# Latent squares, key tiles, cross values and attention banks rearranged in a two-layer hybrid trunk

## The chip, the core and the metric

The kernel runs on one core of one Trainium2 chip. The metric is the device time of one execution in microseconds, and the value compared is the median of several runs. All arithmetic is in float32. A product of two matrices is made of three matmuls in the fp32r form: each operand is split into a high half and the rest, and high times high, high times low and low times high are added up in PSUM.

## What is computed

The reference is a decoder trunk of two layers over 512 tokens of width 1024, with a memory of 256 tokens. Cut to what matters:

```python
h = x
for l in range(2):
    h = h + hybrid_mixer(rmsnorm(h, attn_norm[l]), ...)
    h = h + memory_cross_attention(rmsnorm(h, cross_norm[l]), rmsnorm(mem, mem_norm[l]), ...)
    h = h + squared_relu_mlp(rmsnorm(h, mlp_norm[l]), mlp_w1[l], mlp_w2[l])
return rmsnorm(h, final_norm)

def hybrid_mixer(n, pos, ...):
    proj = n @ w_in          # c_q 256, c_kv 128, k_r 32, then q, k, v of 6 diff heads and of 4 moba heads
    qh  = rmsnorm(c_q, q_norm) @ w_uq        # 6 latent heads, 64 + 32 rotary
    kvh = rmsnorm(c_kv, kv_norm) @ w_ukv     # 64 key, 64 value columns a head
    k_a = concat(k part of kvh, rope(k_r))   # one rotary key for all heads
    o_a = causal_softmax(q_a, k_a) @ v
    lam = exp(sum(lq1*lk1)) - exp(sum(lq2*lk2)) + lam_init
    o_b = rmsnorm((softmax(q1,k1) - lam * softmax(q2,k2)) @ dv, sub_norm) * (1 - lam_init)
    o_c = moba_attention(...)                # with 512 tokens: causal over all blocks
    return concat(o_a, o_b, o_c) @ w_out
```

## The kernel before

The residual stream stands transposed in eight tiles `h` of 128 features x 512 tokens. Weights stream in from HBM through `fetch` (L151) and are split into two halves by `halve`: a copy on ScalarE (L157), the rest by a subtraction (L162) on GpSimd in the mixers, elsewhere wholly or by turns on VectorE. `weights` keeps two blocks ahead in the mixer.

A mixer has two kinds of work that `pipeline` interleaves. *Fill* steps are the projections, in the order "kv cq tok m0 d0 m1 d1 o0 m2 d2 o1 mem cross": the latents (kv, cq: `latent_steps`), the token products (tok: values of two diff pairs and the rotary key, `token_steps`), query, key and value of a latent pair (m: `mla_steps`) and of diff and moba pairs (d, o), and the memory's keys and values (`cross_memory_steps`). *Units* are the attention heads, four query blocks of 128 each, in the order "m0 d0 m1 d1 o0 m2 d2 o1". A unit makes its scores (L638 reads them with the mask or distance added, L640 is the exponent), two units later the probabilities are transposed (L280) and split (L660, L663), and after the last block `mix` (L679, L680 read its bank) multiplies them with the values. A diff head has two maps of scores a unit.

Work that must not stand at once in an engine's queue is put off in *ticks*: each eighth of a projection counts one, a token product 288/512, a latent pair's value and each of its two query products two, its key product one. `after(n, call)` makes the call n ticks later, so the ticks set the place of an instruction in program order. The planner of the framework then orders each engine's instructions by program order and by when it reckons them ready, so a later one may pass an earlier one. Transposes and single matmuls keep their order on TensorE (`hold`), the three matmuls of a product don't.

PSUM has three tags: "mm" with three banks (projections, latent products, cross values), "s" with three (scores, and by `ptags` the mix, tag "o"), "t" with two (transposes, column sums). The token products hold two "mm" and two "s" banks.

The latent query (cq) has two column blocks. Each is copied out (L760) and squared (L762) on ScalarE, the second square is added to the first on VectorE (L764), and `column_sums` multiplies the sum by ones, two columns wide, to get the sums per token. From them the norm's factor is made (GpSimd's power L339 among others), spread over rows by transposes, multiplied in (L782), and split; GpSimd writes the low half (L142).

At the eviction of the token products `rotate` turns the rotary key with seven small VectorE operations (L825 to L828). `turn` transposes it two ticks later, writes it to the first of four key tiles and sends it to three others by DMA (L843). `mla_steps` makes its key product only when the list of key tiles isn't empty. `setup_lambda` (L481 to L489, due at tick 58) reads lam by DMA, and the diff heads use the result. `setup_distances` is due from tick 24.

The cross values are two halves of eight weights each: for every weight the matmuls of both token tiles, each in a bank of its own, both evicted (L144, L145) at the half's end.

Of the kernel before, what the change touches and what calls it, by code (L numbers as in the profile page):

```python
# [101 lines left out]
class Trunk:  # L102
# [251 lines left out]
    def column_sums(self, sq, ones, ntok, w):  # L354

        o = self.psum("t")
        for j in range(ntok):
            self.mm(o[:, j * w:(j + 1) * w], sq[:, j * P:(j + 1) * P], ones, True, True)
        return o
# [10 lines left out]
    def rms_cols(self, sq, ntok, width, bufs, then=None):  # L370
        ms = self.column_sums(sq, self.ones2, ntok, 2)
# [101 lines left out]
    def setup_lambda(self):  # L473
        nc, const = self.nc, self.const
        v = self.tmp()
        nc.sync.dma_start(v[:, :L * 4 * 32], self.a["lam"].to_broadcast([P, L * 4 * 32]))
        prod, dots, ex = self.small(64), self.small(4), self.small(4)
        for l in range(L):
            for j in range(2):
                o = (l * 4 + 2 * j) * 32  # L480
                nc.vector.tensor_tensor(prod[:, :32], v[:, o:o + 32], v[:, o + 32:o + 64], ALU.mult)  # L481
                nc.vector.tensor_reduce(dots[:, 2 * l + j:2 * l + j + 1], prod[:, :32], mybir.AxisListType.X, ALU.add)
        nc.scalar.activation(ex, dots, AF.Exp)
        self.neg_lam = const.tile([P, L], F32, name="neg_lam")
        for l in range(L):
            li = 0.8 - 0.6 * math.exp(-0.3 * l)
            nl = self.neg_lam[:, l:l + 1]
            nc.vector.tensor_tensor(nl, ex[:, 2 * l + 1:2 * l + 2], ex[:, 2 * l:2 * l + 1], ALU.subtract)
            nc.vector.tensor_scalar_sub(nl, nl, li)  # L489
# [139 lines left out]
    def scores(self, i, terms, bias, slope):  # L629

        nc = self.nc
        n = (i + 1) * P
        s = self.psum("s")
        for j, (q, k) in enumerate(terms):
            self.mm(s[:, :n], q[:, i * P:n], k[:, :n], j == 0, j == len(terms) - 1, hold=False)
        t = self.tmp()
        st = self.small(2)
        nc.vector.tensor_tensor_reduce(out=t[:, :n], in0=s[:, :n], in1=bias, scale=-slope, scalar=TOP,  # L638
                                       op0=ALU.add, op1=ALU.min, accum_out=st[:, 0:1])
        nc.scalar.activation(t[:, :n], t[:, :n], AF.Exp, bias=st[:, 0:1], scale=-1.0, accum_out=st[:, 1:2])  # L640
        return t, st[:, 1:2]
# [45 lines left out]
    def head_units(self, maps, bias, slope, v, e, o, mixed, done=None):  # L687


        nc = self.nc  # L690
        st = {}

        def start(i):
            n = (i + 1) * P
            got = [self.scores(i, terms(), bias(i), slope) for terms in maps]
            t, sm = got[0]
            if len(maps) == 1:
                r = self.small(1)
                nc.vector.reciprocal(r, sm)
                (nc.gpsimd if i == 1 else nc.vector).tensor_scalar_mul(t[:, :n], t[:, :n], r)  # L700
            else:
                t2, s2 = got[1]
                nc.vector.scalar_tensor_tensor(t[:, :n], t2[:, :n], mixed(i, sm, s2), t[:, :n], ALU.mult, ALU.add)  # L703
# [38 lines left out]
    def mixer(self, l):  # L742
# [9 lines left out]
        def latent_steps(srcs, gain, width):  # L752


            cs = []
            sq = None
# [12 lines left out]
            def columns():  # L769
                ms = self.column_sums(sq, self.ones2, NQ, 2)  # L770
# [21 lines left out]
        def token_steps():  # L792

            n = 2 * P + 32
            ps = [self.psum("mm"), self.psum("mm"), self.psum("s"), self.psum("s")]
# [9 lines left out]
            def evict():  # L805
                vs = []
# [24 lines left out]
            def turn(t):  # L831
# [64 lines left out]
        def mla_units(p, got):  # L896
# [74 lines left out]
        def pair_units(p, got):  # L971
# [20 lines left out]
            def r1():  # L992
                if "r1" not in oo:
                    oo["r1"] = self.sb.tile([P, 2 * NQ], F32, tag="r1", name=self.name("r1"), bufs=2)
                return oo["r1"]

            def mixed(e):
                def factor(i, s1, s2):
# [3 lines left out]
                    nc.vector.reciprocal(r1()[:, 2 * i + e:2 * i + e + 1], s1)  # L1002
                    return r[:, 1:2]
                return factor

            def done_diff():

                ot, r = o(), r1()
# [3 lines left out]
                def columns():  # L1012
                    ms = self.column_sums(sq, self.halves, NQ, 2)
# [33 lines left out]
        self.keys = []  # L1047
# [121 lines left out]
    def cross_memory_steps(self, l):  # L1169
# [246 lines left out]
    def run(self):  # L1416
# [3 lines left out]
        self.ptags = {"o": "s"}  # L1420
# [11 lines left out]
        self.chain_n, self.chain_l, self.chain_d, self.chain_k = 6, 12, 4, 2  # L1432
# [135 lines left out]
```

## Time and profile before

| | |
|---|---|
| median of 3 runs | 1529.4 us (1529.02 to 1532.49) |
| profiled execution | 1527.16 us |
| its span, first to last instruction | 1525.3 us |
| TensorE busy | 1481.2 us, 97% |
| VectorE busy | 1060.3 us, 70% |
| ScalarE busy | 856.9 us, 56% |
| GpSimd busy | 365.3 us, 24% |
| mean granted TensorE clock | 0.994 |

Layer 0 runs to about 772 us and layer 1 from there. In each the mixer takes the first quarter thousand microseconds or so, then come the output projection, the cross attention and the feed-forward part. A row of the timeline gives the start and the length of a group of like instructions on one engine, and in brackets how long the engine stood idle before it and which instruction ended that.

### The profile page before, as it was taken

To read this page: it belongs to the slowest core of one execution; us is meant where nothing else is said; L and a number is where in the kernel's file an instruction comes from. 1 tells how busy PE (TensorE), PEld (TensorE's weight loads), DVE (VectorE), ACT (ScalarE), POOL (GpSimd) and SP (SyncE) were. 2 spreads that over 40 slices of the span, in tenths; PEclk is the share of its full clock that TensorE was granted. 3 is DMA by queue.
4 is the path that set the end of the run, shared out by engine and by line. 5 is a ranking of instruction groups with operands and counts; after the bars stand their busy time and mean duration, and the time that the engine had idled before them with its cause. 6 is when DMAs were issued, how large, how long until landed. Compare 5 with 4: busy or idle time off the path is not lost.

```text
span 1525.3 us, 24601 instructions
## 1 busy us (share of the span) xinstructions
PE 1481.2 (97%) x8648; PEld 1295.4 (85%) x8648; DVE 1060.3 (70%) x2422; ACT 856.9 (56%) x1887; POOL 365.3 (24%) x302
## 2 busy tenths in 40 slices
PE   7899999999999999999999999999999999999997
PEld 6778897888899899998897888878888989899887
DVE  7688888536699666675537898873378976677753
ACT  5666777535566544454446677764366654445441
POOL 2645375442000000000145446644400000000001
PEclk9999999999999999999999999999999999999998
DMA  4434543231223323322224535423212332333331
GB/s 153 127 106 138 153 132 111 77 96 49 87 74 125 111 88 105 100 96 98 96 77 112 150 113 154 118 86 95 98 34 76 106 123 90 104 96 106 111 97 55
DMA packets 90139, 157.24 MB, mean 103 GB/s; under 512 B 12065, under 2 KB 17057, under 8 KB 90017
## 3 DMA queue, kind: packets, MB, share of 16 engines
q1 hardware_dynamic: 89728, 155.63, 33.2%
q8 instruction: 68, 1.11, 0.3%
q14 instruction: 55, 0.44, 0.1%
q10 hardware_dynamic: 288, 0.05, 0.0%
HBM read 136.24 MB, written 2.10 MB: 91 GB/s over the span
## 4 chain that ended last, share of the span: by engine, by line
PE 71%; DVE 10%; issue 9%; ACT 4%; DMA 3%; POOL 2%; SPq 0%; POOLq 0%; DVEq 0%; ACTq 0%
PE mm L277 58%; PE s L277 10%; PE t L280 2%; DMA raw<-w 2%; DVE tmp L638 1%; ACT tmp L640 1%; DVE tmp L703 1%; POOL w L162 1%; DVE pt L663 1%; ACT B L140 1%; DMA raw<-w_in 1%; DVE small L1001 1%; POOL B L142 1%; PE t L277 1%; DVE tmp L261 1%
## 5 line engine op out<-in xcount | busy, mean ns | idle before, releaser
L277 PE MATMUL mm<-B,w 128*128 128x512 f32 (+1 forms) x2490 | 574.4, 386 | 1.3 <-POOL B L142 1.3
L277 PEld LDWEIGHTS mm<-B,w 128*128 128x128 f32 x2490 | 453.0, 189 | 95.1 <-POOL B L142 2.6
L277 PE MATMUL mm<-A,w 128*128 128x512 f32 (+1 forms) x1920 | 386.7, 351 | 6.2 <-ACT A L144 5.8
L157 ACT CAST w<-raw 128x512 fp32r<-128x512 f32 (+1 forms) x372 | 225.1, 607 | 269.6 <-PE mm L277 208.0
L277 PEld LDWEIGHTS mm<-A,w 128*128 128x128 f32 x1920 | 311.8, 190 | 50.7 <-ACT A L144 5.8
L162 POOL TENSOR_TENSOR w<-raw,w 128x512 fp32r<-128x512 f32 (+2 forms) x180 | 228.0, 1273 | 220.1 <-ACT w L157 177.9
L410 POOL TENSOR_TENSOR tmp<-tmp,tmp 128x512 f32<-128x512 f32 (+1 forms) x25 | 30.8, 1234 | 655.7 <-ACT tmp L407 653.6
L162 DVE TENSOR_TENSOR w<-raw,w 128x512 fp32r<-128x512 f32 x192 | 134.4, 700 | 35.5 <-ACT w L157 35.2
L640 ACT ACTIVATE tmp<-tmp,small 128x384 f32<-128x384 f32 (+3 forms) x176 | 99.0, 562 | 66.0 <-DVE small L638 63.2
L1080 DVE TENSOR_TENSOR h<-mm,h 128x512 f32<-128x512 f32 x92 | 63.3, 688 | 70.9 <-PE mm L277 70.6
L140 ACT CAST B<-tmp 128x512 fp32r<-128x512 f32 (+2 forms) x156 | 91.9, 591 | 24.1 <-DVE tmp L680 4.8
L277 PE MATMUL mm<-pt,B 128*128 128x256 f32 x768 | 102.9, 283 | 2.4 <-ACT tmp L1319 2.4
L277 PEld LDWEIGHTS mm<-pt,B 128*128 128x128 f32 x768 | 95.8, 189 | 3.4 <-ACT tmp L1319 3.4
L261 DVE TENSOR_TENSOR tmp<-raw,raw 128x512 f32<-128x512 f32 x64 | 44.0, 688 | 65.9 <-DMA raw<-w 65.9
L264 ACT CAST B<-tmp 128x512 fp32r<-128x512 f32 x96 | 59.5, 620 | 50.8 <-DVE tmp L261 50.8
L142 DVE TENSOR_TENSOR B<-tmp,B 128x512 fp32r<-128x512 f32 (+1 forms) x110 | 75.5, 686 | 12.3 <-ACT B L140 8.3
L280 PE MATMUL t<-ident,tmp 128*128 128x128 f32 (+1 forms) x444 | 74.5, 274 | 9.3 <-DVE tmp L828 3.3
L280 PEld LDWEIGHTS t<-ident,tmp 128*128 128x128 f32 (+1 forms) x444 | 54.2, 140 | 24.8 <-issue 4.2
L142 POOL TENSOR_TENSOR B<-tmp,B 128x512 fp32r<-128x512 f32 (+1 forms) x46 | 61.4, 1340 | 49.7 <-ACT B L140 47.4
L663 DVE TENSOR_TENSOR pt<-t,pt 128x256 fp32r<-128x256 f32 (+1 forms) x192 | 67.1, 370 | 6.3 <-ACT pt L660 5.4
L277 PE MATMUL s<-pt,B 128*128 128x512 f32 (+3 forms) x352 | 71.0, 345 | 0.0
L339 POOL TENSOR_TENSOR small<-small,mhalf 128x4 f32<-128x4 f32 (+2 forms) x19 | 23.4, 1229 | 198.2 <-DVE small L373 174.5
(195 smaller groups left out, 2135.8 us busy)
## 6 DMA issues: line engine op xcount, KB each, us to landing
raw<-w SPq DMA_DIRECT2D x256, 256.0 KB, 2.9
raw<-w_in SPq DMA_DIRECT2D x64, 256.0 KB, 3.0
st<-B SPq DMA_DIRECT2D x144, 64.0 KB, 2.0
raw<-w_ck SPq DMA_DIRECT2D x32, 256.0 KB, 2.9
raw<-w_cv SPq DMA_DIRECT2D x32, 256.0 KB, 2.7
raw<-w_out SPq DMA_DIRECT2D x32, 256.0 KB, 2.7
raw<-w_cq SPq DMA_DIRECT2D x32, 256.0 KB, 2.7
raw<-w_co SPq DMA_DIRECT2D x32, 256.0 KB, 2.6
```

The lines of the kernel that those rows point to most:

```text
L140: nc.scalar.copy(hi, x)
L142: eng.tensor_tensor(lo, x, hi.bitcast(F32), ALU.subtract)
L157: self.nc.scalar.copy(w[:, 0, :], raw)
L162: eng.tensor_tensor(w[:, 1, :], raw, w[:, 0, :].bitcast(F32), ALU.subtract)
L261: nc.vector.tensor_tensor(got[name], x, y, op)
L264: nc.scalar.copy(w[:, 0, :], raw)
L277: self.in_order(self.nc.tensor.matmul(out, lhs, rhs, start=start, stop=stop, skip_group_check=open), hold)
L280: self.in_order(self.nc.tensor.transpose(out, x, self.ident))
L410: eng.tensor_tensor(s[:, :n], s[:, :n], self.sq[:, :n], ALU.add)
L640: nc.scalar.activation(t[:, :n], t[:, :n], AF.Exp, bias=st[:, 0:1], scale=-1.0, accum_out=st[:, 1:2])
L663: nc.vector.tensor_tensor(lo, src, hi.bitcast(F32), ALU.subtract)
L1080: nc.vector.tensor_tensor(self.h[m], ps, self.h[m], ALU.add)
```

## The change

- `column_sums` takes a list of square tiles and adds them up in PSUM; the latents hand over both squares and the add on VectorE goes.
- `setup_lambda` works on all pairs at once and is due at tick 44 instead of 58; the distances are due from tick 28 instead of 24.
- The exponent's sums of the first map of a diff head go straight to the tile that held their reciprocals; one reciprocal of eight columns is taken when the pair is done.
- The multiply of the probabilities of block 1 runs on VectorE instead of GpSimd.
- The token products use three "s" banks and one "mm" bank.
- The four key tiles are allocated at the eviction of the token products; the turn comes six ticks after the rotation instead of two, and a latent head's scores wait, in program order, for the turn.
- In the cross values the second token tile runs two weights behind the first.
- The mix takes a bank of tag "mm" instead of "s".

```diff
-    def column_sums(self, sq, ones, ntok, w):
+    def column_sums(self, sqs, ones, ntok, w):
         o = self.psum("t")
         for j in range(ntok):
-            self.mm(o[:, j * w:(j + 1) * w], sq[:, j * P:(j + 1) * P], ones, True, True)
+            for i, sq in enumerate(sqs):
+                self.mm(o[:, j * w:(j + 1) * w], sq[:, j * P:(j + 1) * P], ones, i == 0, i == len(sqs) - 1)
...
-        prod, dots, ex = self.small(64), self.small(4), self.small(4)
-        for l in range(L):
-            for j in range(2):
-                o = (l * 4 + 2 * j) * 32
-                nc.vector.tensor_tensor(prod[:, :32], v[:, o:o + 32], v[:, o + 32:o + 64], ALU.mult)
-                nc.vector.tensor_reduce(dots[:, 2 * l + j:2 * l + j + 1], prod[:, :32], mybir.AxisListType.X, ALU.add)
+        prod, dots, ex = self.small(128), self.small(4), self.small(4)
+
+        pairs = v[:, :L * 4 * 32].rearrange("p (g f d) -> p g f d", f=2, d=32)
+        prod = prod.rearrange("p (g d) -> p g d", d=32)
+        nc.vector.tensor_tensor(prod, pairs[:, :, 0, :], pairs[:, :, 1, :], ALU.mult)
+        nc.vector.tensor_reduce(dots, prod, mybir.AxisListType.X, ALU.add)
...
-        st = self.small(2)
+        st = self.small(1)
...
-        nc.scalar.activation(t[:, :n], t[:, :n], AF.Exp, bias=st[:, 0:1], scale=-1.0, accum_out=st[:, 1:2])
-        return t, st[:, 1:2]
+        nc.scalar.activation(t[:, :n], t[:, :n], AF.Exp, bias=st[:, 0:1], scale=-1.0, accum_out=sums)
+        return t
...
-                (nc.gpsimd if i == 1 else nc.vector).tensor_scalar_mul(t[:, :n], t[:, :n], r)
+                nc.vector.tensor_scalar_mul(t[:, :n], t[:, :n], r)
...
                 s = self.tmp()
                 nc.scalar.activation(s, c, AF.Square)
-                if sq is not None:
-                    nc.vector.tensor_tensor(s, s, sq, ALU.add)
-                sq = s
+                sqs.append(s)
                 cs.append(c)
...
-                ms = self.column_sums(sq, self.ones2, NQ, 2)
+                ms = self.column_sums(sqs, self.ones2, NQ, 2)
...
-            ps = [self.psum("mm"), self.psum("mm"), self.psum("s"), self.psum("s")]
+            ps = [self.psum(t) for t in ("s", "s", "s", "mm")]
...
             def evict():
+                self.keys += [self.pair("B") for _ in range(4)]
...
-                first = self.pair("B")
+                first = self.keys[0]
                 self.split(first[64:128, 0, :], first[64:128, 1, :], u[64:128, :], kind="kr")
-                self.keys.append(first)
-                for j in range(3):
-                    kt = self.pair("B")
+                for kt in self.keys[1:]:
                     nc.sync.dma_start(kt[64:128].bitcast(F32), first[64:128].bitcast(F32))
-                    self.keys.append(kt)
+                self.turned = True
...
                 def terms(e=e):
+                    while not self.turned:
+                        self.tick()
...
-                    nc.vector.reciprocal(r1()[:, 2 * i + e:2 * i + e + 1], s1)
...
-                ot, r = o(), r1()
+                ot, r = o(), self.small(8)
+                nc.vector.reciprocal(r, sums())
...
             ps = [self.psum("mm") for t in range(2)]
-            for k in range(KT):
-                w = self.weights(a["w_cv"][l, c * KT + k])
-                for t in range(2):
-                    ts = slice(t * P, (t + 1) * P)
-                    self.mm3(ps[t], (mem[k][0][:, ts], mem[k][1][:, ts]), (w[:, 0, :], w[:, 1, :]),
-                             k == 0, k == KT - 1)
-                    yield 640
+            ws = []
+            for j in range(KT + 2):
+                if j < KT:
+                    ws.append(self.weights(a["w_cv"][l, c * KT + j]))
+                for t, k in ((0, j), (1, j - 2)):
+                    if 0 <= k < KT:
+                        ts, w = slice(t * P, (t + 1) * P), ws[k]
+                        self.mm3(ps[t], (mem[k][0][:, ts], mem[k][1][:, ts]), (w[:, 0, :], w[:, 1, :]),
+                                 k == 0, k == KT - 1)
+                        yield 640
...
-        self.ptags = {"o": "s"}
+        self.ptags = {"o": "mm"}
...
-        self.chain_n, self.chain_l, self.chain_d, self.chain_k = 6, 12, 4, 2
+        self.chain_n, self.chain_l, self.chain_d, self.chain_k = 6, 12, 4, 6
...
-            self.after(24 + 2 * n, part)
-        self.after(58, self.setup_lambda)
+            self.after(28 + 2 * n, part)
+        self.after(44, self.setup_lambda)
```

## Rows read from the trace of the kernel before

**Rows 1.** Page, part 1: busy us (share of the span), instructions by engine.

```profile
PE 1481.2 (97%) x8648; PEld 1295.4 (85%) x8648; DVE 1060.3 (70%) x2422; ACT 856.9 (56%) x1887; POOL 365.3 (24%) x302
```

**Rows 2.** TensorE's waits, whole span: us in total, times, longest.

```profile
PE s L277 <- DVE small L638: 4.1, 6, 1.2
PE s L277 <- DVE tmp L680: 3.4, 7, 0.7
PE t L280 <- DVE tmp L828: 3.3, 2, 2.4
PE t L277 <- DVE tmp L764: 2.9, 1, 2.9
...
PE t L280 <- DVE tmp L700: 2.4, 1, 2.4
...
PE mm L277 <- DVE B L145: 2.2, 2, 1.1
...
PE t L280 <- POOL tmp L700: 1.2, 1, 1.2
```

**Rows 3.** Stretches: us, PE, PEld, DVE, ACT, POOL busy, PEclk, DMA share, GB/s.

```profile
40.50:42.00 1.50, 1.50 (x8) 1.50 (x7) 1.49 (x4) 1.10 (x2) 0.85 (x1) 0.50 0.15 57
...
39.00:44.00 5.00, 5.00 (x29) 5.00 (x28) 3.83 (x10) 2.48 (x5) 3.40 (x4) 0.66 0.27 69
76.50:81.50 5.00, 5.00 (x18) 4.20 (x19) 4.63 (x14) 2.13 (x6) 1.01 (x1) 0.66 0.32 76
807.00:812.00 5.00, 5.00 (x18) 4.01 (x18) 2.39 (x4) 2.97 (x5) 2.56 (x2) 0.66 0.31 82
```

**Rows 4.** TensorE's timeline, first 60 us: start, us, instructions [idle before <-releaser].

```profile
29.43 0.67 PE L277 MATMUL mm<-w,A 128*128 128x288 f32 x3 [0.67 <-ACT tmp L760]
...
37.29 1.02 PE L277 MATMUL t<-ones,tmp 128*128 128x2 f32 x8 [2.86 <-DVE tmp L764]
...
51.06 0.97 PE L277 MATMUL mm<-B,w 128*128 128x512 f32 x3 [0.71 <-POOL B L142]
52.32 2.11 PE L277 MATMUL mm<-B,w 128*128 128x512 f32 x8 [0.29 <-POOL B L142]
```

**Rows 5.** TensorE by line and shape, two-column sums: count | busy us, mean ns.

```profile
L277 PE MATMUL t<-ones,tmp 128*128 128x2 f32 x92 | 11.1, 241 | 4.6 <-DVE tmp L764 2.9 <-DVE tmp L410 1.7
```

**Rows 6.** ScalarE's timeline, 18 to 58 us.

```profile
32.88 0.63 ACT L762 ACTIVATE tmp<-tmp 128x512 f32<-128x512 f32 x1
```

**Rows 7.** GpSimd's timeline, 18 to 58 us.

```profile
49.74 2.53 POOL L142 TENSOR_TENSOR B<-tmp,B 128x512 fp32r<-128x512 f32 x2
```

**Rows 8.** VectorE's timeline, 56 to 84 us.

```profile
71.27 0.19 DVE L481 TENSOR_TENSOR small<-tmp 128x32 f32<-128x32 f32 x1 [1.39 <-DMA tmp<-lam]
...
73.92 0.69 DVE L638 CUSTOM_DVE_ANT_0 tmp<-s,causal 128x512 f32<-128x512 f32 x1
```

**Rows 9.** VectorE's timeline, 797 to 822 us.

```profile
802.80 0.22 DVE L826 TENSOR_TENSOR tmp<-tmp,nsin 128x64 f32<-128x64 f32 x1
...
803.08 1.32 DVE L827 TENSOR_TENSOR tmp<-tmp,tmp 128x64 f32<-128x64 f32 x1
...
820.22 1.39 DVE L700 TENSOR_SCALAR tmp<-tmp,small 128x384 f32<-128x384 f32 x1
```

**Rows 10.** GpSimd's timeline, 797 to 822 us.

```profile
802.96 1.36 POOL L162 TENSOR_TENSOR w<-raw,w 128x512 fp32r<-128x512 f32 x1 [0.68 <-ACT w L157]
...
820.11 1.29 POOL L142 TENSOR_TENSOR B<-tmp,B 128x512 fp32r<-128x512 f32 x1 [0.28 <-ACT B L140]
```

**Rows 11.** The same view, the mixers' 25 us in which VectorE is fullest.

```profile
175.00:200.00 25.00, 24.07 (x161) 21.59 (x161) 22.94 (x66) 18.71 (x50) 14.51 (x12) 1.00 0.68 189
```

**Rows 12.** TensorE's timeline, 222 to 275 us.

```profile
231.14 1.48 PE L277 MATMUL s<-pt,B 128*128 128x512 f32 x8
```

**Rows 13.** VectorE's timeline, 222 to 275 us.

```profile
235.92 0.69 DVE L680 TENSOR_TENSOR tmp<-s,tmp 64x512 f32<-64x512 f32 x1
```

More of the change, by code (lines that the diff above doesn't have):

```diff
@@ L370, in rms_cols @@
     def rms_cols(self, sq, ntok, width, bufs, then=None):
-        ms = self.column_sums(sq, self.ones2, ntok, 2)
+        ms = self.column_sums([sq], self.ones2, ntok, 2)
         v = self.small(NQ)
@@ L476, in setup_lambda @@
         nc.sync.dma_start(v[:, :L * 4 * 32], self.a["lam"].to_broadcast([P, L * 4 * 32]))
-        prod, dots, ex = self.small(64), self.small(4), self.small(4)
-        for l in range(L):
-            for j in range(2):
-                o = (l * 4 + 2 * j) * 32
-                nc.vector.tensor_tensor(prod[:, :32], v[:, o:o + 32], v[:, o + 32:o + 64], ALU.mult)
-                nc.vector.tensor_reduce(dots[:, 2 * l + j:2 * l + j + 1], prod[:, :32], mybir.AxisListType.X, ALU.add)
+        prod, dots, ex = self.small(128), self.small(4), self.small(4)
[3 more added lines that the diff above has]
+        nc.vector.tensor_reduce(dots, prod, mybir.AxisListType.X, ALU.add)
         nc.scalar.activation(ex, dots, AF.Exp)
         self.neg_lam = const.tile([P, L], F32, name="neg_lam")
+        nc.vector.tensor_tensor(self.neg_lam, ex[:, 1::2], ex[:, 0::2], ALU.subtract)
         for l in range(L):
-            li = 0.8 - 0.6 * math.exp(-0.3 * l)
             nl = self.neg_lam[:, l:l + 1]
-            nc.vector.tensor_tensor(nl, ex[:, 2 * l + 1:2 * l + 2], ex[:, 2 * l:2 * l + 1], ALU.subtract)
-            nc.vector.tensor_scalar_sub(nl, nl, li)
+            nc.vector.tensor_scalar_sub(nl, nl, 0.8 - 0.6 * math.exp(-0.3 * l))
     def setup_rotary(self):
@@ L627, in stacks, with scores @@
         return tiles, calls
-    def scores(self, i, terms, bias, slope):
+    def scores(self, i, terms, bias, slope, sums):
         nc = self.nc
@@ L694, in start @@
             n = (i + 1) * P
-            got = [self.scores(i, terms(), bias(i), slope) for terms in maps]
-            t, sm = got[0]
             if len(maps) == 1:
-                r = self.small(1)
+                sm, r = self.small(1), self.small(1)
+                t = self.scores(i, maps[0](), bias(i), slope, sm)
                 nc.vector.reciprocal(r, sm)
-                (nc.gpsimd if i == 1 else nc.vector).tensor_scalar_mul(t[:, :n], t[:, :n], r)
+                nc.vector.tensor_scalar_mul(t[:, :n], t[:, :n], r)
             else:
-                t2, s2 = got[1]
-                nc.vector.scalar_tensor_tensor(t[:, :n], t2[:, :n], mixed(i, sm, s2), t[:, :n], ALU.mult, ALU.add)
+                s1, s2 = mixed.sums(i), self.small(1)
+                t, t2 = (self.scores(i, terms(), bias(i), slope, s) for terms, s in zip(maps, (s1, s2)))
+                nc.vector.scalar_tensor_tensor(t[:, :n], t2[:, :n], mixed(s1, s2), t[:, :n], ALU.mult, ALU.add)
             st[i] = t
@@ L752, in latent_steps @@
         def latent_steps(srcs, gain, width):
-            cs = []
-            sq = None
+            cs, sqs = [], []
             for j, src in enumerate(srcs):
@@ L990, in terms, with sums, factor @@
                 return [(q, k[e]) for k in got["k"]]
[L992 to L995, printed above, removed]
+            def sums():
+                if "sums" not in oo:
+                    oo["sums"] = self.sb.tile([P, 2 * NQ], F32, tag="r1", name=self.name("r1"), bufs=2)
+                return oo["sums"]
             def mixed(e):
-                def factor(i, s1, s2):
+                def factor(s1, s2):
                     r = self.small(2)
@@ L1001, in factor @@
                     nc.vector.scalar_tensor_tensor(r[:, 1:2], r[:, 0:1], self.neg_lam[:, l:l + 1], s1, ALU.mult, ALU.mult)
-                    nc.vector.reciprocal(r1()[:, 2 * i + e:2 * i + e + 1], s1)
                     return r[:, 1:2]
+                factor.sums = lambda i: sums()[:, 2 * i + e:2 * i + e + 1]
                 return factor
             def done_diff():
-                ot, r = o(), r1()
+                ot, r = o(), self.small(8)
+                nc.vector.reciprocal(r, sums())
                 sq = self.tmp()
@@ L1012, in columns @@
                 def columns():
-                    ms = self.column_sums(sq, self.halves, NQ, 2)
+                    ms = self.column_sums([sq], self.halves, NQ, 2)
                     vv, f = self.small(8), self.small(8)
@@ L1046, in mixer @@
         got = {n: {"moves": []} for n in "d0 d1 d2 m0 m1 m2 o0 o1".split()}
-        self.keys = []
+        self.keys, self.turned = [], False
         steps = {"kv": kv_steps, "cq": cq_steps, "tok": token_steps}
```

## The prediction

> **What bounds the kernel now.** I read the engines' busy time first: TensorE is busy for 97% of the span and no other engine for more than 70% [rows 1]. So only two things can make this kernel faster: less TensorE work, or fewer of its idle microseconds. The change takes no TensorE work away, it adds some. So the second view is the list of what TensorE waited for, and the reader is to see that nearly every wait in it that is not at the two ends of the program names an operation that this diff touches [rows 2]. They add up to 19.5 us: 7.5 us on score banks (L638 and L680 are the readers that free one), 3.3 on the rotary key's turn (L828), 2.9 on the latent sum (L764), 2.4 and 1.2 on a multiply of the probabilities (L700, once on VectorE and once on GpSimd), 2.2 on the cross values' eviction (L145). The third view is the granted clock in short stretches. In the five microseconds shortly behind each of the three longest of these waits (2.9 us on L764, 2.4 on VectorE's L700, 2.4 on L828) it is 0.66 in the mean, and within the first of them it stands at 0.50, which is 1.2 GHz in place of 2.4 [rows 3]. TensorE is at work there, so each time 5 x 0.34 = 1.7 us of its work is lost. So a long wait costs itself plus 1.7 us, and the pool to be won is 19.5 + 5.1 = 24.6 us, 1.6% of the time.
>
> **Part by part, against the profiled execution's 1527.16 us.**
>
> Latent squares on TensorE. Removed: one 128x512 add on VectorE a layer (L764) behind which the column sums wait. Added: four more matmuls of two columns a layer. Each is two instructions in the trace (eight for four at 37.29 [rows 4]), and one costs 11.1 / 92 = 0.12 us [rows 5], so 8 x 0.12 = 0.97 us a layer on the bounding engine. In layer 1 there is no wait on the add, so there it is a plain loss: +1.0. In layer 0 the sums wait for 2.9 us. The second square ends at 32.88 + 0.63 = 33.5 us on ScalarE [rows 6], and TensorE was out of work at 37.29 - 2.86 = 34.4, so without the add this wait goes, and its slow clock with it. The 0.67 us at 29.43 (a token product waiting for a projection bank to be copied out) goes with the token products' new banks, "s" thrice and "mm" once. That is 2.86 + 1.71 + 0.67 - 0.97 = 4.3 us. But the next consumer is the first query product at 51.06 and 52.32, which already waits for GpSimd to write the low half of the latents [rows 4]: two of these in 2.53 us, ending at 52.27 [rows 7]. GpSimd has the weights' halves in the same queue, and its two latent operations can move forward only as far as the column sums and the distances' operations do (sums from 37.3 to about 34.4, so 2.9 us, and the distances are now due four ticks later, out of the way in part). I take 3.0 us won, between 0 (the GpSimd queue holds everything) and 5.3 (4.3 plus the two waits of 1.0 that exist now).
>
> Lambda, earlier and in fewer instructions. Now VectorE stands idle 1.39 us for the DMA of lam and then does eight small operations; the 128x512 score reader that waits behind them starts only at 73.92 [rows 8], its exponent and its multiply come after, and TensorE waits 2.4 us for that multiply. With lambda due at tick 44 instead of 58 nothing of it is left there: 2.4 + 1.7 = 4.1 us won. It goes to where the first query products run. The lam DMA then queues on SP among weight fetches, and VectorE, and ScalarE behind it with the exponent, may stand there instead. From below the price is 0, from above the same 1.39 us; I take 0.4 since VectorE's order is made anew around it. Net 3.7.
>
> Multiplies of the second block (i = 1) from GpSimd to VectorE, 20 of them. One wait of 1.2 us names the GpSimd form [rows 2]. I take 0.6 of it as won, from 0 to 1.2. Here a row speaks against the change: the 128x384 multiply on VectorE took 1.39 us from 820.22 while GpSimd was in an operation from 820.11 to 821.40 [rows 9, 10], and the add at 803.08 took 1.32 us where its neighbour took 0.22, ending as GpSimd's operation from 802.96 did. The Trainium skill ("SBUF — State Buffer", "Who interferes with whom") says that such VectorE operations and GpSimd share a port pair that one holds for its whole instruction while the other stands still, and the trace agrees with it. By it alone the move makes 20 more VectorE instructions that can be stopped this way. Measured by the row, at most about a microsecond each on VectorE, and TensorE sees it only where VectorE is the last to arrive.
>
> Reciprocals: 48 single-column ones become six of eight columns. Off the path. They and the multiplies about cancel on VectorE, and I cost them at nothing; what hides them is VectorE's own slack, 2 us of 25 in its fullest stretch of a mixer [rows 11]. If that is gone, the first rival below holds.
>
> Attention outputs in the projections' banks. The waits for score banks are 4.1 + 3.4 = 7.5 us [rows 2], because the mix of a head takes one of three "s" banks while two maps of scores need two. With the mix out of "s" these waits have no cause except VectorE being late anyway. The new price is on "mm". The mix at 231.14 holds its bank until L680 ends at 236.6, 4.0 us after its last matmul [rows 12, 13]. A projection step takes longer than that, so three banks do for one projection and one mix. They are short where a latent query, key and value run one behind the other, and during the cross values, which hold two. I take 5.0 won and 1.0 lost again, net 4.0; ends are 7.5 won and 2 lost.
>
> Cross values skewed. The wait of 1.1 us at the seam between the two halves, once a layer, is for the first half's eviction [rows 2]. With the second token tile two weights behind, the first bank is finished two steps sooner. Against it: two more weight tiles stay in use out of five, and at the start of each half the weights go twice as fast, with GpSimd making them. From -2.2 to +2.2 (the same wait at the weights instead); I take -1.2.
>
> Keys at the eviction, the turn at tick 6. Value, first and second query product each count two ticks, so the turn is now called just behind the second query product. That is where the trace already has it, between the query products and the key product. TensorE waits there because the seven rotary operations on VectorE end late, and two of the adds stand behind GpSimd [rows 9, 10]. Those weight halves remain. So I leave the 0.9 us of layer 0 and the 2.4 + 1.7 us of layer 1 where they are: 0, from -5.0 to +1.7. The SP queue's three key copies move with the turn; the weights fetched behind them have landed early enough in neither layer to matter more than they do now.
>
> Sum: +1.0 - 3.0 - 3.7 - 0.6 - 4.0 - 1.2 = -11.5 us: 1515.7 for a profiled execution. The median of the runs, 1529.4, stands 2.2 us above the profiled one, so the forecast is **1517.9 us**. Its own range is 1513 to 1523.
>
> **Rivals.** (a) The turn's wait in layer 1 goes too, since the order around it is made anew and the two adds fall between GpSimd's operations: 4.1 us more, 1513.8. For it: nothing but 2.2 us of standing still makes the wait. Against it: the same operations remain. 0.20. (b) VectorE becomes the bound in the mixers. It is at 22.9 of 25 us there in the fullest stretch [rows 11]; shorten TensorE's side and take 20 multiplies in, and half of the gains come back as waits on L638, L663 and L700: -5.7, 1523.7. 0.17. (c) The change doesn't do what it says: the engines' order comes out so that the latent sums, lambda and the seam wait as before for something else in the same queue, and only some bank waits go while the added matmuls stay: about -2, 1527. 0.10. (d) Slower: all 32 mixes (16 heads a layer) now queue for a projection's bank. A bank is held 4.0 us after a mix. If a mix waits 0.9 us in the mean, 32 x 0.9 = 29 us are lost and 17 us remain after the gains: 1546. It turns slower than now from 0.36 us a mix, and by a measurable amount from 0.5 us. For it: three banks and two held during the cross values. Against it: the score banks, used more often than these, cost only 7.5 us in all today. 0.06.
>
> **How the numbers follow.** Forecast 0.47, (a) 0.20, (b) 0.17, (c) 0.10, (d) 0.06. A measurement of this kernel can tell about 0.3% (4.6 us) from no change: faster is below 1524.8, slower above 1534.0. Faster gets the forecast, (a) and two thirds of (b): 0.78. The same gets the rest of (b) and (c): 0.16. Slower 0.06. The range takes in (a) with the low ends of the unknown costs and (b) and (c) up to the point where 2 in 10 is left out: 1508.5 to 1528.
>
> **What would show it.** Right: no TensorE wait on L764 and none of 2 us near 76 us; one dip of the clock left, at the turn in layer 1; waits for "s" banks under 3 us in all; eight more two-column instructions a layer; the first query product some 3 us sooner. Wrong: a wait of over 2 us at the first query product on GpSimd's latents; "mm" matmuls of a mix waiting on a projection's reader; "w" waits at the start of the cross values; VectorE over 23 of 25 us where it is 22.9 now.

## The result and the profile after

The changed kernel takes 1548.05 us (median of 6 runs, 1546.47 to 1548.71). The kernel before, beside it, takes 1529.07 (6 runs). The ratio is 1.0124, with a 95% interval of 1.0108 to 1.0139: the change costs 19 us where 11.5 were forecast as won. The profiled execution took 1546.96 us, with a span of 1545.1 against 1525.3, so 19.8 us are to be found in the two traces.

The engines' busy time, part 1 of the page of the kernel after, answers to [rows 1]; the two-column sums, from the groups by line and shape, answer to [rows 5]:

```profile
PE 1491.0 (96%) x8664; PEld 1303.5 (84%) x8664; DVE 1065.7 (69%) x2391; ACT 856.7 (55%) x1887; POOL 343.1 (22%) x282
...
L277 PE MATMUL t<-ones,tmp 128*128 128x2 f32 x108 | 13.3, 245 | 2.4 <-DVE tmp L411 1.7 <-ACT tmp L762 0.6
```

TensorE has the 16 two-column instructions more that the diff adds (108 against 92, 2.2 us), yet it is busy for 9.8 us longer, and idle for 10.0 us longer (54.1 against 44.1). One half of the loss is therefore waits, and most of the other half work at a slower clock (worked out at the end of the part on the prediction). TensorE's waits over the whole span (us in total, times, longest), to be read beside [rows 2]:

```profile
PE s L277 <- DVE small L638: 10.5, 15, 1.5
PE mm L277 <- ACT A L144: 5.8, 1, 5.8
PE t L280 <- DVE small L344: 3.1, 2, 1.5
PE mm L277 <- ACT w L157: 2.9, 3, 1.3
PE t L280 <- DVE pt L663: 2.8, 5, 0.8
PE t L280 <- DVE tmp L1032: 2.6, 2, 1.3
...
PE s L277 <- POOL B L142: 2.2, 2, 1.6
PE t L280 <- DVE tmp L827: 1.9, 2, 1.0
...
PE mm L277 <- POOL w L162: 1.5, 3, 0.6
...
PE t L277 <- ACT tmp L762: 0.6, 1, 0.6
```

Some line numbers shift by one or two between the kernels (L638 to L700 don't): L827 here is L828 of the kernel before, and L829 in the run with the turn alone. Every wait that the forecast named, but for the score banks', is gone or smaller: L764, L700 and L680 are not in the list, the turn's has gone from 3.3 to 1.9 us. In their place stand waits that the trace of before does not have (L344, L157), and the score banks' waits on L638 have gone from 4.1 + 3.4 to 10.5 us although the mixes left those banks. The granted clock in stretches (us, PE, PEld, DVE, ACT, POOL busy, PEclk, DMA share, GB/s), the first four of the five in which it is low (the fifth runs from about 820.8 to 824.1 us), then the one that answers to [rows 11] and layer 1's fullest:

```profile
267.80:274.50 6.70, 5.03 (x21) 4.13 (x20) 4.67 (x17) 3.10 (x8) 1.64 (x1) 0.50 0.00 0
1022.20:1032.20 10.00, 7.35 (x27) 5.92 (x28) 7.13 (x27) 4.13 (x14) 1.64 (x1) 0.50 0.00 0
32.30:39.00 6.70, 6.70 (x29) 6.70 (x30) 4.87 (x18) 0.87 (x2) 3.50 (x4) 0.50 0.29 81
127.90:131.10 3.20, 3.20 (x12) 2.61 (x12) 2.06 (x8) 1.63 (x6) 3.08 (x3) 0.50 0.58 177
...
175.00:200.00 25.00, 23.58 (x160) 21.19 (x158) 22.50 (x64) 18.05 (x47) 11.93 (x9) 1.00 0.66 186
...
935.00:960.00 25.00, 23.51 (x167) 21.68 (x166) 23.35 (x68) 18.55 (x50) 11.36 (x9) 1.00 0.57 161
```

At 0.50 (1.2 GHz) half of the busy time is lost work, so the first two stretches cost 5.03 / 2 = 2.5 and 7.35 / 2 = 3.7 us. They lie at the same place of the two layers, just ahead of the output projection. VectorE is at 22.5 of 25 us in the stretch of [rows 11], less than before, and at 23.35 in layer 1's fullest, where the kernel before has 22.96 in its own (875 to 900 us).

To place the loss I set marks in both traces (first token product, last cross value, a block of the output projection added to `h`, and so on; in layer 0 it is the eighth and last block, in layer 1 the sixth, and from either block to the other both kernels take 10.99 us) and took the lengths between them. This is worked out, no view of the profile:

```
us from mark to mark                           before   after  difference
start to the end of layer 0's token products    48.78   47.53        -1.3
to the first cross value                       175.01  176.54        +1.5
cross values, layer 0                           34.53   35.21        +0.7
to the output projection's eighth block         55.49   60.37        +4.9
to layer 1's first token product               471.25  471.54        +0.3
token products, layer 1                         14.58   15.46        +0.9
to the first cross value                       168.78  174.72        +5.9
cross values, layer 1                           34.82   35.17        +0.4
to the output projection's sixth block          44.51   50.21        +5.7
to the end                                     477.60  478.39        +0.8
```

More than half, 10.6 us, lies between the last cross value and the output projection; most of the rest, 1.5 and 5.9 us, lies between the token products and the cross values. TensorE's timeline there, first before, then after (start, us, instructions, idle before and its releaser):

```profile
261.43 0.94 PE L277 MATMUL mm<-B,w 128*128 128x512 f32 x3
263.00 0.61 PE L277 MATMUL s<-st,st 128*128 128x384 f32 x2 [0.63 <-DVE tmp L680]
...
265.04 1.64 PE L277 MATMUL mm<-B,w 128*128 128x512 f32 x6
...
269.37 2.09 PE L277 MATMUL mm<-B,w 128*128 128x512 f32 x8
...
273.21 1.48 PE L277 MATMUL s<-pt,B 128*128 128x512 f32 x8
```

```profile
263.52 0.72 PE L277 MATMUL s<-st,st 128*128 128x512 f32 x2 [1.19 <-DVE small L638]
264.08 0.95 PE L277 MATMUL t<-halves,tmp 128*128 128x2 f32 x8
265.32 0.30 PE L280 MATMUL t<-ident,tmp 128*128 128x128 f32 x1 [0.29 <-DVE pt L663]
266.46 0.44 PE L280 MATMUL t<-ident,tmp 128*128 128x128 f32 x2 [0.83 <-DVE pt L663]
266.65 1.68 PE L277 MATMUL mm<-pt,B 128*128 128x512 f32 x8
268.13 0.86 PE L280 MATMUL t<-ident,tmp 128*128 128x128 f32 x3
270.53 2.31 PE L280 MATMUL t<-ident,tmp 128*128 128x128 f32 x8 [1.54 <-DVE small L344]
272.49 2.43 PE L277 MATMUL mm<-pt,B 128*128 128x512 f32 x8
274.75 5.49 PE L277 MATMUL mm<-B,w 128*128 128x512 f32 x23
```

The lines `mm<-B,w` of before are products of the output projection. They stand ahead of the last mix (273.21) and fill TensorE while the last heads go through ScalarE and VectorE. After the change there is none of them until 274.75, behind the last mix: TensorE waits 1.19 + 0.29 + 0.83 us, runs at 1.2 GHz from about 267.8 us, and waits 1.54 us more. The reader is to see that nothing in these lines waits for an "mm" bank at run time. I read it as the order itself: a bank is given out in program order, all mixes come before the output projection in program order, and its products can't be put ahead of a mix that has the bank first. The lines alone don't prove that; the runs below that change only the last mixes' bank test it. In the kernels' order on TensorE, 26 matmuls of the output projection stand before the last mix of each layer in the kernel before, and none in the kernel after.

### The profile page after: what moved, and what is told of

It reads as the page before. It is cut to its first block, busy times and chain, and to the rows that moved or that the text cites. A ratio compares the mean times of both kernels' runs of the same rounds, so it can differ in the third digit from the quotient of the medians.

```text
span 1545.1 us, 24547 instructions
## 1 busy us (share of the span) xinstructions
PE 1491.0 (96%) x8664; PEld 1303.5 (84%) x8664; DVE 1065.7 (69%) x2391; ACT 856.7 (55%) x1887; POOL 343.1 (22%) x282
## 5 line engine op out<-in xcount | busy, mean ns | idle before, releaser
L157 ACT CAST w<-raw 128x512 fp32r<-128x512 f32 (+1 forms) x372 | 224.5, 606 | 272.5 <-PE mm L277 223.9
L277 PE MATMUL mm<-pt,B 128*128 128x256 f32 (+3 forms) x1120 | 176.7, 306 | 2.3 <-ACT tmp L1324 2.3
L277 PEld LDWEIGHTS mm<-pt,B 128*128 128x128 f32 x1120 | 156.6, 192 | 9.8 <-ACT tmp L1324 3.3
L640 ACT ACTIVATE tmp<-tmp,small 128x384 f32<-128x384 f32 (+3 forms) x176 | 98.7, 561 | 77.9 <-DVE small L638 77.6
L140 ACT CAST B<-tmp 128x512 fp32r<-128x512 f32 (+1 forms) x156 | 92.2, 591 | 28.4 <-DVE tmp L877 8.0
L280 PE MATMUL t<-ident,tmp 128*128 128x128 f32 (+1 forms) x444 | 78.0, 284 | 12.9 <-DVE small L344 3.1
L142 DVE TENSOR_TENSOR B<-tmp,B 128x512 fp32r<-128x512 f32 (+1 forms) x110 | 81.0, 736 | 9.4 <-ACT B L140 5.5
L663 DVE TENSOR_TENSOR pt<-t,pt 128x256 fp32r<-128x256 f32 (+1 forms) x192 | 67.1, 371 | 6.4 <-ACT pt L660 5.1
L660 ACT CAST pt<-t 128x256 fp32r<-128x256 f32 (+1 forms) x192 | 57.8, 333 | 17.1 <-PE t L280 16.1
```

Source lines behind the costliest of these rows:

```text
L140: nc.scalar.copy(hi, x)
L142: eng.tensor_tensor(lo, x, hi.bitcast(F32), ALU.subtract)
L157: self.nc.scalar.copy(w[:, 0, :], raw)
L277: self.in_order(self.nc.tensor.matmul(out, lhs, rhs, start=start, stop=stop, skip_group_check=open), hold)
L280: self.in_order(self.nc.tensor.transpose(out, x, self.ident))
L660: nc.scalar.copy(hi, src)
```

## The experiments

Two theories stood against each other. **T**: the loss is the banks', and in them the lost cover at the end of each mixer. **R**: it comes from the small moves (cross values skewed, VectorE taking more work, a new turn), or from mixes queueing among the projections as in rival (d). Ratios are to the kernel before on the same chip; "after" and "before" ahead of a diff say from which kernel it starts.

**Mix back in the score banks** (after):

```diff
-        self.ptags = {"o": "mm"}
+        self.ptags = {"o": "s"}
```

> The changed kernel with the mix back in a bank of tag s, all else as changed. Theory: the mix took the projections' banks away from the output projection, whose products stood among the last heads' instructions before (26 matmuls a layer) and stand behind the last mix now (none); with the tail of TensorE empty its clock falls too. Then this run wins about 5 us a layer, 10 us in all, against the changed kernel: 1538 us, with no slow clock at the ends of the mixers. Rival (the bank move pays, as I forecast, and something else lost): this run is 4 us slower than the changed kernel, 1552.

1536.11 us, 1.0051 (1.0034 to 1.0068): 11.9 us of the 19 come back. The stretches from the last cross value to the marked block of the output projection are 54.54 and 43.53 us, shorter than before, and 26 of its matmuls stand ahead of the last mix again. So the bank is the largest part, but not all.

**Mix in the projections' banks alone** (before, the same line the other way):

> The kernel before with this one edit alone, the mix in a bank of tag mm. Theory: 10 us slower than before, 1539, with waits and a slow clock at the end of both mixers and nowhere else. Rival, my forecast: 4 us faster than before, 1525.

1548.93, 1.0124 (1.0092 to 1.0157): by itself it costs as much as the whole change: 20.8 us by the two medians (1528.14 beside it), 14 to 24 by the ratio's interval. The two end stretches are 8.2 and 8.0 us longer than before, and one matmul of the output projection is left before the last mix.

**Cross values not skewed** (after):

```diff
-            for j in range(KT + 2):
+            for j in range(KT):
...
-                for t, k in ((0, j), (1, j - 2)):
+                for t, k in ((0, j), (1, j)):
```

> The changed kernel with the cross values as before, both token tiles at every weight. Theory that the skew costs by itself (weights wanted twice as fast): 2 to 3 us faster than the changed kernel, 1545. Rival, that it is neutral or a small gain: 1548 to 1550.

1548.46, 1.0127 (1.0102 to 1.0151): no difference to the changed kernel that this can tell.

**Latent squares added on VectorE again** (after):

```diff
+                if sqs:
+                    nc.vector.tensor_tensor(s, s, sqs.pop(), ALU.add)
                 sqs.append(s)
```

> The changed kernel with the second latent square added on VectorE again and one column sum. Theory: the eight added two-column instructions cost 1.0 us a layer and bring the slow clock of 6.8 us at 32 us on, where before 3.4 us stood; without them layer 1 wins 1 us, and layer 0 has the wait on the add again with 3.4 us of slow clock: about 1547. Rival, my forecast that they pay 2 us net: 1550.

1549.99, 1.0138 (1.0114 to 1.0162): 1.9 us worse than the changed kernel, with overlapping intervals. The sign and the size are those of the forecast's two terms (-3.0 and +1.0); the run alone doesn't prove them.

**Bank and skew undone** (after, both edits above):

> The changed kernel with the mix in s banks and the cross values unskewed. With the bank put back the cross values' stretch still took 1.7 us (layer 0) and 3.2 us (layer 1) longer than before, most of it slow clock behind waits for weights. Theory that this is the skew's doubled demand for weights: about 4 us faster than with the bank alone put back, 1532 us, each stretch within 0.5 us of before. Rival (chance of the clock): 1536.

1533.92, 1.0035 (1.0021 to 1.0050): 2.2 us less than with the bank alone undone, so the skew costs about that where the mixes are in "s" (again with overlapping intervals). The traces point the same way: the cross values take 36.20 and 37.99 us in the two layers with the skew, 34.78 and 34.81 without it. A loss of 5 us against before is still there. Of the edits that could cost it, the multiplies, the turn and the reciprocals are left; the first two are undone next.

**The same, multiplies of block 1 back on GpSimd:**

```diff
-                nc.vector.tensor_scalar_mul(t[:, :n], t[:, :n], r)
+                (nc.gpsimd if i == 1 else nc.vector).tensor_scalar_mul(t[:, :n], t[:, :n], r)
```

> As the run with bank and skew put back, and the multiplies of block 1 back on GpSimd. Theory A, that these 20 multiplies on VectorE make the middle of the mixers slow (5.4 and 3.7 us between the token products and the cross values, with the bank put back): 5 to 9 us faster than without this, 1525 us or less. Theory B, that the keys and the turn do: no difference. Theory C, that it is the planner's new order as a whole: something between.

**The same, key tiles and turn as before** (multiplies on VectorE):

```diff
-                self.keys += [self.pair("B") for _ in range(4)]
...
-                first = self.keys[0]
+                first = self.pair("B")
...
-                for kt in self.keys[1:]:
+                self.keys.append(first)
+                for j in range(3):
+                    kt = self.pair("B")
...
-        self.chain_n, self.chain_l, self.chain_d, self.chain_k = 6, 12, 4, 6
+        self.chain_n, self.chain_l, self.chain_d, self.chain_k = 6, 12, 4, 2
```

The lines that let a latent head's scores wait for the turn stay in; they have nothing left to do, since the key product, which the scores need, again waits for the list of key tiles that the turn fills.

> As the run with bank and skew put back, and the key tiles and the turn as before (turn two ticks after the rotation). Theory A (the multiplies): the turn's wait of 2.4 us and its slow clock come back in layer 1, 3 us slower or the same. Theory B (the keys allocated early and the first scores waiting for the low half of the queries, 1.6 us in layer 1): 3 to 5 us faster.

1527.34, 0.9989 (0.9979 to 0.9998), with the multiplies back, and 1526.57, 0.9986 (0.9977 to 0.9995), with the turn back. Either one undone gives 6.6 or 7.4 us back. That is more than each can cost alone, as the next run shows.

**The front alone** (before, with the latent squares in PSUM, the token products in "s", "s", "s", "mm", and the new lambda and due times; multiplies, turn, skew, mix and reciprocals as before):

```diff
-            ps = [self.psum("mm"), self.psum("mm"), self.psum("s"), self.psum("s")]
+            ps = [self.psum(t) for t in ("s", "s", "s", "mm")]
...
-        self.after(58, self.setup_lambda)
+        self.after(44, self.setup_lambda)
```

> The kernel before with three edits alone: latent squares summed on TensorE, token products in three s banks and one mm bank, lambda earlier and in fewer instructions with the distances later. My forecast's terms for these give -3.0 + 1.0 - 3.7: 5.7 us faster than before, 1523 us, with the layer 0 wait on the latent sum and the wait near 76 us gone. Rival: the planner's new order gives it back behind the first heads, 1528.

1525.06 (10 runs), 0.9974 (0.9965 to 0.9983): 3.7 us faster than the kernel before, the fastest of all. Two waits of before are gone from its trace; these are its rows for what was 2.86 us at 37.29 [rows 4]:

```profile
29.86 0.28 PE L277 MATMUL t<-ones,tmp 128*128 128x2 f32 x2
30.89 1.72 PE L277 MATMUL t<-ones,tmp 128*128 128x2 f32 x14 [0.75 <-ACT tmp L761]
```

From here, the multiplies cost 1526.57 - 1525.06 = 1.5 us, the turn 1527.34 - 1525.06 = 2.3, and both 1533.92 - 1525.06 = 8.9 (the reciprocals, which these three also have and which no run has alone, are in each). They don't add up. The next four runs measure each edit from the kernel before, and ask where in the mixer the banks cost.

**Mixes in "mm", but in "s" when no projection is left to fill with** (after):

```diff
-        ps = self.psum("o")
+        ps = self.psum("o" if self.fill.todo else "s")
```

> The changed kernel, but a mix that comes when no projection is left to fill with takes a bank of tag s; all other mixes keep mm. These are the last two or three heads of each layer, with 26 matmuls of the output projection standing before the last mix in TensorE's order again, where the changed kernel has none. If the loss of the bank move lies only at the end of each mixer, the time is what it is with all mixes in s: 1536, so 1534 to 1539. If the forecast was also right that the other mixes gain by leaving s (4 us), 1532. If the mixes among the projections lose as well by waiting for a projection's bank, most of the 12 us stay: 1543 or more.

**The same in the kernel before** (mixes in "mm", the last ones in "s"):

> The kernel before with the mixes in mm, but those that come when no projection is left in s as before. All mixes in mm cost 20.8 us on this kernel, of which the stretches from the cross values' end to the output projection's end show 16.2. If the end of the mixers is the whole cause: 1527 to 1531, no change; if the forecast's term holds for the other mixes, 1525. If the mixes among the projections lose too, 1533 to 1536 (the 4.6 us that the ends do not show, or more).

1537.09, 1.0053 (1.0040 to 1.0067), and 1531.47, 1.0022 (1.0010 to 1.0034). The last mixes alone account for 1548.05 - 1537.09 = 11.0 us of the changed kernel's loss, and 1548.93 - 1531.47 = 17.5 of the 20.8 that the bank costs alone. Both kernels have 26 matmuls of the output projection ahead of the last mix again, in each layer. All other mixes in "mm" cost 1.0 and 2.9 us: no gain, and a small loss, which in the second run is clear of noise (1.5 to 5.2 us by the interval). In the first of the two, the stretch that was at 0.50 runs with TensorE always busy, at the full clock:

```profile
268.00:277.00 9.00, 8.99 (x51) 7.33 (x50) 6.61 (x23) 4.89 (x13) 1.64 (x1) 1.00 0.00 0
1020.00:1030.00 10.00, 10.00 (x55) 8.11 (x54) 7.27 (x27) 4.69 (x14) 1.64 (x1) 1.00 0.00 0
```

So T holds for the bank, and rival (d)'s queue among the projections does not. The waits of the second run tell why the score banks gave nothing; the first line is of its list of waits, the second of its timeline at one place, the other two of the kernel before at the same place:

```profile
PE s L277 <- DVE small L638: 10.9, 12, 1.9
...
237.41 0.39 PE L277 MATMUL s<-st,st 96*128 96x256 f32 x1 [1.87 <-DVE small L638]
```

```profile
233.65 0.33 PE L277 MATMUL s<-st,st 96*128 96x128 f32 x1 [0.92 <-DVE small L638]
...
236.67 0.72 PE L277 MATMUL s<-st,st 96*128 96x256 f32 x2 [0.24 <-DVE tmp L680]
```

The waits on L680 have become waits on L638, and grown. TensorE is not held at the first block's scores any more (0.92 us before), comes to the next block's sooner, and waits there for VectorE to read the scores before (1.87 us against 0.92 + 0.24). It is not a matter of order: of 496 score matmuls only 14 stand further ahead among the projections than in the kernel before.

**Multiplies on VectorE alone** (before):

> The kernel before with only the multiplies of block 1 on VectorE. The forecast has -0.6: 1528. With the front edits in, this alone cost 1.5: 1530. If the multiplies are harmful by themselves (they cost 6.6 with the turn moved), 1535.

1533.52, 1.0033 (1.0021 to 1.0046): 5.0 us slower (3.2 to 7.0 by the interval), at the end where it is harmful by itself. The trace shows one place with 2.05 us that the kernel before does not have. These are VectorE's, GpSimd's and TensorE's timelines:

```profile
134.92 0.16 DVE L699 RECIPROCAL small<-small 128x1 f32<-128x1 f32 x1 [0.97 <-ACT tmp L640]
135.00 0.83 DVE L343 SCALAR_TENSOR_TENSOR small<-small 128x8 f32<-128x8 f32 x1
135.75 1.45 DVE L700 TENSOR_SCALAR tmp<-tmp,small 128x256 f32<-128x256 f32 x1
137.13 1.24 DVE L344 TENSOR_TENSOR small<-small,small 128x8 f32<-128x8 f32 x1
...
139.29 0.68 DVE L607 TENSOR_TENSOR B<-t,B 128x512 fp32r<-128x512 f32 x1
```

```profile
135.76 1.30 POOL L142 TENSOR_TENSOR B<-tmp,B 128x512 fp32r<-128x512 f32 x1
137.01 1.33 POOL L162 TENSOR_TENSOR w<-raw,w 128x512 fp32r<-128x512 f32 x1
```

```profile
140.12 0.30 PE L280 MATMUL t<-ident,tmp 128*128 128x128 f32 x1 [2.05 <-DVE B L607]
```

The moved multiply, 0.34 us where nothing disturbs it (at 79.88 of the same trace), takes 1.45 and ends at 137.20, GpSimd's operation of 135.76 at 137.06. The next operation, which reads two tiles of eight columns, takes 1.24 and ends at 138.37, GpSimd's of 137.01 at 138.34. The Trainium skill ("SBUF — State Buffer", "Who interferes with whom") has this as a port pair that VectorE and GpSimd share, and that one of them holds for a whole instruction while the other stands still; the rows agree, the ends lie within 0.14 us of each other. Not all of it is the edit's: in the kernel before the operation of L344 takes 1.21 us too (at 132.98), behind a GpSimd operation of its own. New are the 1.45 us of the multiply and 0.97 us for which VectorE stood idle for the exponent (L640) just before. Over the whole trace, 4 of the 20 moved multiplies take over 1.0 us (1.02 to 1.45), the other 16 less than 0.5.

The trace does not show where the rest of the 5.0 us is. When it comes to the first moved multiply (69.24 us on VectorE), this execution is already 1.9 us behind that of the kernel before, after the same instructions in the same order on every engine up to there: the clock is at 0.50 from about 51.2 to 58.0 us, where the kernel before has it at 1.00. That part can't be the multiplies'.

**Key tiles and turn alone** (before):

> The kernel before with only the key tiles at the eviction and the turn six ticks after the rotation. The forecast has 0: 1529. With the front edits in, this alone cost 2.3: 1531. If the turn is harmful by itself (it cost 7.4 with the multiplies moved), 1536; if the later turn takes the wait of layer 1 away, 1525.

1531.73, 1.0021 (1.0013 to 1.0030): 3.2 us slower, near what its loss on the front alone (2.3) had said. TensorE's timeline at the turn in layer 1 and at the first latent scores in layer 0:

```profile
808.89 0.63 PE L280 MATMUL t<-ident,tmp 128*64 128x128 f32 x4 [2.22 <-DVE tmp L829]
```

```profile
63.32 0.73 PE L277 MATMUL s<-B,B 128*128 128x128 f32 x4 [2.28 <-POOL B L142]
```

The turn's wait in layer 1 stays, as forecast (2.22 us, 2.43 before), and a new one of 2.28 us appears in layer 0 where the scores need the low half from GpSimd's queue; the kernel before waits 0.21 us for it there, and 0.90 for layer 0's turn, which no longer shows. From the token products to the cross values the trace is 1.5 us longer in layer 0 and 2.1 in layer 1. The loss in layer 1 isn't at the turn; its waits on L638 are 2.1 us against 0.5 there, and why is not shown.

## Why the prediction was wrong

**The bank term failed.** It was -4.0, with ends at -7.5 and +2; it measured +11.9 with the rest in place and +20.8 alone. Two steps of it were wrong. The first: "with the mix out of 's' these waits have no cause except VectorE being late anyway". VectorE is late: 7.5 us of waits became 10.5. The second: the price on "mm" was worked out as the time that a bank is held at run time (4.0 us), with the query products and the cross values as the places where banks are short. The place that decides is behind them, where the last mixes stand in front of the output projection in program order: 26 of its matmuls covered the last heads of each layer before, none after, and that alone is 11.0 of the 11.9 us and 17.5 of the 20.8. That the projection's products cover the last heads could be read in the trace of before, in the `mm<-B,w` lines from 261.43 on, but I had looked for waits, and cover leaves no wait. The range missed it for the same reason.

Rival (d) named this bank and gave 1546, and the time came out near it. Its mechanism (0.9 us for each of 32 mixes) is not what the runs show: with the last mixes in "s", the rest lose 1.0 or 2.9 us in all.

**Multiplies: -0.6 forecast, +5.0 alone, 1.5 to 6.6 beside other edits.** The sentence that spoke against the move was right in its mechanism and was then priced at nothing, since "TensorE sees it only where VectorE is the last to arrive". It is the last to arrive at the place shown above; how much of the 5.0 us such places make up isn't shown.

**Turn: 0 forecast, +3.2 alone.** With this edit alone the wait stayed, which was right (in the kernel with all the edits it is 1.0 us at the longest). That the edit also brings a latent head's first scores to wait for the low half of their operand was left out, though the end of +1.7 had room for part of it. With both, the loss is 8.9 and not the sum. In the trace of the kernel with both, two waits stand in layer 0's mixer, 1.83 us on L663 and 1.61 on L680, that the kernel without the multiplies doesn't have. Why they need both edits isn't settled.

**Skew: -1.2 forecast; nothing to +2.2 measured.** The bad end, "the same wait at the weights instead", came true: 1.1 us a layer for L145 became 1.28 + 0.62 for the weights' halves, in each layer:

```profile
244.76 0.73 PE L277 MATMUL mm<-w,A 128*128 128x512 f32 x2 [1.28 <-ACT w L157]
246.11 1.20 PE L277 MATMUL mm<-w,A 128*128 128x512 f32 x4 [0.62 <-POOL w L162]
```

**The front won, but less, and not by all of its terms:** +1.0 - 3.0 - 3.7 = -5.7 forecast, -3.7 measured (-2.6 to -5.4 by the interval). The waits on L764 and at 76 us went, and the 16 two-column instructions cost 2.2 us against the 1.94 of the sum. In the trace of the front alone the lambda term came out: no long wait near 76 us, and the clock is at 1.00 from 76.5 to 81.5. The latent term hardly shows at the query products: the token products end 2.9 us sooner (45.85 against 48.78), but the row that answers to 51.06 starts at 50.91, since TensorE waits 0.98, 0.88 and 1.20 us ahead of it for halves of the latents from GpSimd and ScalarE. That is near the term's bad end, where GpSimd's queue holds everything; the run that undoes this edit alone (1.9 us worse, with overlapping intervals) leaves open what it is worth. In the kernel after, the same row is 1.2 us sooner, not 3, and its waits on GpSimd stand as they did:

```profile
49.88 0.97 PE L277 MATMUL mm<-B,w 128*128 128x512 f32 x3 [0.78 <-POOL B L142]
51.12 2.11 PE L277 MATMUL mm<-B,w 128*128 128x512 f32 x8 [0.27 <-POOL B L142]
```

**The clock.** A wait was priced at itself plus 1.7 us. The trace of after has five low stretches ahead of the last products, before had three, and the forecast left one. Half of the busy time in them is 13.2 us after and 5.1 before: 8 of the 19.8 us are work done at 1.2 GHz. The 1.7 us didn't go with a wait either. The front alone has neither the wait on L764 nor the one near 76 us, for each of which 1.7 us were counted as won, and it still has three low stretches, two of them at other places (from about 33.6 to 36.9, 50.7 to 54.0 and 805.0 to 808.3 us).

## What to carry to other kernels

A tile pool whose buffers are given out in program order is also an order: whoever takes a buffer earlier in the program holds back all later work of that tag, even where no wait on it shows in the trace. Before an operation is moved to another pool, look at what the planner has lifted past it, which shows as useful work in the place of a wait. Edits that each cost or bring 1 to 5 us on a kernel that is 97% busy don't add up, so measure them singly and keep those that win (here the front, 3.7 us).

## What the runs showed of the hardware

The clock fell behind shorter waits than the three of before. In the kernel after it is at 0.50 from about 32.3 us, and ahead of it stand only these: 0.65 us of waiting and two-column matmuls.

```profile
30.07 0.28 PE L277 MATMUL t<-ones,tmp 128*128 128x2 f32 x2
31.00 2.04 PE L277 MATMUL t<-ones,tmp 128*128 128x2 f32 x14 [0.65 <-ACT tmp L762]
```

The kernel with the last mixes in "s" has the same instructions in the same order on TensorE up to about 263 us and waited 0.75 us there, yet its clock is at 1.00 in that stretch and falls a little later, behind another wait:

```profile
32.30:39.00 6.70, 6.70 (x53) 6.70 (x53) 5.23 (x17) 2.32 (x5) 3.71 (x5) 1.00 0.43 120
48.20:54.80 6.60, 6.11 (x17) 4.18 (x17) 6.41 (x20) 3.21 (x12) 3.70 (x3) 0.50 0.35 108
```

So which of several short waits is followed by the low clock differs between two executions of the same order, and a term of one such stretch (3.4 us at the most here, half of 6.70) can't be put down to one edit from one trace. The two at the end of the mixers, 2.5 and 3.7 us, are of another kind: they stand where the cover is gone, and in the kernel with the cover back neither is there.
